# An encoder layer with attention and a Hyena branch on one core: GpSimd's sums ahead of the attention moved to VectorE, and half of the weights' low parts made by an accumulating DMA

## The chip, the cores and the metric

The kernel runs on one core of a Trainium2 chip. The metric is the device time of one execution in microseconds (us), as the median of several runs. A core has TensorE (PE in the profile, with PEld for its weight loads), VectorE (DVE), ScalarE (ACT), GpSimd (POOL) and SyncE (SP). Each engine works through its own list of instructions in order and waits on semaphores for the others. DMAs are issued from the lists of SP, ACT and POOL and run on 16 shared DMA engines.

## The reference, cut to what matters

One layer on x of 512 positions by 1024 features, all in fp32:

```
proj = rmsnorm(x) @ w_in                      # 1024 -> q-latent 768 | kv-latent 256 | rope key 32 | Hyena 1536
q = rmsnorm(c_q) @ w_uq ; k, v = rmsnorm(c_kv) @ w_ukv   # 8 heads, q and k normed, 32 features rotated
y_attn  = softmax(q k^T * s) v
x0, x1, vh = split(dwconv3(u_h))
h_fwd, h_bwd = filters(three sin layers of a small MLP, then filt_w_out)
y_hyena = x0 * (circular convolution of x1*vh with the filters, by FFT)
x = x + concat(rmsnorm(y_attn), rmsnorm(y_hyena)) @ w_out
x = x + (silu(g) * u) @ w_down    with g, u = dwconv3(rmsnorm(x) @ w_up)
x = x + sigmoid(x @ w_ple_gate) * rmsnorm(p @ w_ple)
```

## The kernel before, in words

Features lie on the 128 partitions and the 512 positions along the free dimension. To keep fp32 accuracy, every operand of a large product is split in two: a high part, rounded to the fp32r format that TensorE reads, and a low part, the operand minus that. A product of K tiles is three matmuls for each tile: high by high, high by low and low by high (`prod3`).

**Weights** come as tiles of 128 x 1024 (w_uq: 128 x 768), in the order in which TensorE uses them (`stream`): 21 of w_in, one of w_ukn, six of w_uq, one of w_ukv, eight of w_out, then w_up, w_down, w_ple and w_gate. `wload` (L134) brings one in: SP loads the raw tile `wr` (L136), ScalarE rounds it into `wh` (L139), and the low part `wl` is the difference. The table CUTS gives for each of the first 37 tiles the column up to which VectorE subtracts (L141); GpSimd takes the rest (L143). There are three buffers for `wr` and two each for `wh` and `wl`; when TensorE starts on tile i, tiles up to i+1 have been ordered (L167). So a tile may be prepared once TensorE has left the tile two ahead of it. From w_up on, VectorE makes all of `wl`.

**Stages.** 1. x is loaded, scaled and split, and its sum of squares is gathered in accx and accy (L485 to L491), on GpSimd for even k and on VectorE for odd k. 2. `in_gemm` (L310) runs the 21 tiles of w_in: kv-latent, rope key, then eight Hyena tiles whose short convolution (`conv`, L532) is on ScalarE and VectorE, and whose products x1*vh (`uu`) and their sums (`pq`) are on GpSimd (L625 to L629), four more Hyena tiles, and six of the q-latent, whose squares are summed in accx (L645). 3. Between them run tasks: the filter network (`filter_task`, L394) with three sin layers (L367 on TensorE, L370 to L372 on VectorE, L374 on ScalarE), the sums of the two halves of filt_w_out (L403, GpSimd; the loaded tile takes a `wr` buffer), and the filters (L436); the transforms (`transform_task`, L545): sums at L574 to L577, products with the filters at L586 to L591, sums at L595, L596 and L607. 4. The products with w_ukn and w_uq, the squares of each head (`square`, L650) and the scales (`key_task`, `query_scale`; rows are turned by TensorE at L228), rotations (`rotate`, L353). 5. Attention, eight heads by four blocks of 128 queries, the normalization by GpSimd (L866), with the values, the inverse transform and the first parts of w_out between. 6. w_out, the gated MLP and the last gate.

**What sets the order.** TensorE's order is written out by the program: a clock counts the cost of the matmuls written so far, and a task goes on when its time has come (`advance`, `spawn`). The lists of the other engines are ordered by a list scheduler with priorities, from the program order and its own estimates. The table ENG names the engine for single operations by a key, and `e(key, default)` looks it up.

The functions that the change touches and what calls them, with the line numbers of the profile:

Of the kernel before, what the change touches and what calls it, by code (L numbers as in the profile page):

```python
# [12 lines left out]
F32 = mybir.dt.float32  # L13
# [33 lines left out]
D_FT = 3.5  # L47
CUTS = [0, 0, 1024, 256, 512, 512, 256, 768, 256, 768, 256, 0, 512, 0, 256, 256, 768, 256, 512, 0, 256, 512, 0, 512, 768, 512, 768, 768, 0, 256, 256, 256, 0, 256, 0, 512, 512]
TAIL = 'E0 P E1 R O S0 S1 V0 V1 S2 S3 V2 G0 V3'
ENG = {'pr0': 'G', 'a53': 'V', 'a64': 'V', 'sp3': 'V', 'pr2': 'G', 'sp7': 'G', 'qa2': 'V', 'm5': 'V', 'a51': 'G', 'ah1': 'G', 'hl0': 'V', 'fwo': 'G', 'ah3': 'G', 'qa5': 'V', 'hl2': 'G', 'qa3': 'V', 'm6': 'V', 'm7': 'G', 'm2': 'V', 'qa1': 'V', 'sp5': 'G', 'xt': 'V', 'Uc': 'G', 'sp4': 'G', 'w01': 'V', 'w11': 'V', 'a61': 'G', 'pr3': 'G', 'a67': 'G', 'a63': 'V', 'u4': 'G', 'a65': 'G', 'w10': 'G', 'u3': 'G', 'sp0': 'G', 'eos': 'V', 'vx': 'A', 'vl': 'V', 'vh': 'V', 'va': 'V', 'vf': 'V', 've': 'V', 'vc': 'A', 'sx': 'A', 'sl': 'V', 'sh': 'V', 'sa': 'V', 'sf': 'V', 'se': 'V', 'sc': 'V', 'qa4': 'G', 'sp6': 'V', 'm4': 'V', 'rot2': 'G', 'cv5': 'V', 'm1': 'G', 'a62': 'V', 'rot1': 'G'}  # L50
PRI = {'val': 20, 'kt': 60, 'rms': -120, 'cols': 400, 'H': 0, 'gate': 150, 'uT': -120, 'io': -20, 'sq': 20, 'turn': 0, 'so': -300, 'fold': -120, 't8': 0, 'gsq': -50, 'ie': 400}
QACT = 1
# [34 lines left out]
def tile_encoder_block(  # L87
# [6 lines left out]
    V, S, G, PE, SP = nc.vector, nc.scalar, nc.gpsimd, nc.tensor, nc.sync  # L94

    def e(key, default):
        return {"V": V, "G": G}[ENG.get(key, default)]

# [24 lines left out]
    def f32(ap):  # L123
        return ap.bitcast(F32)
# [9 lines left out]
    def wload(src, n, cut):  # L134
        raw = wpool.tile([P, 1024], F32, tag="wr", name="wr", bufs=3)
        SP.dma_start(raw[:, :n], src)  # L136
        hi = wpool.tile([P, 1024], F32R, tag="wh", name="wh")
        lo = wpool.tile([P, 1024], F32R, tag="wl", name="wl")
        S.activation(hi[:, :n], raw[:, :n], AF.Copy)  # L139
        if cut:  # L140
            V.tensor_tensor(lo[:, :cut], raw[:, :cut], f32(hi[:, :cut]), op=ALU.subtract)  # L141
        if cut < n:
            G.tensor_tensor(lo[:, cut:n], raw[:, cut:n], f32(hi[:, cut:n]), op=ALU.subtract)  # L143
        return hi, lo

    stream = [(w_in[m], 1024, CUTS[m]) for m in range(21)]
    stream += [(w_ukn, 1024, CUTS[21])] + [(w_uq[m], 768, CUTS[22 + n]) for n, m in enumerate(UQ)] + [(w_ukv, 1024, CUTS[28])]
    stream += [(w_out[1, m], 1024, CUTS[29 + m]) for m in range(4)] + [(w_out[0, m], 1024, CUTS[33 + m]) for m in range(4)]
    stream += [(w_up[m], 1024, 1024) for m in range(2 * NFF)]
# [8 lines left out]
    def ahead(i):  # L158
        while len(ready) < min(i, len(stream)):
            with tc.high_priority(offset=WPRI if len(ready) > 3 else 0):  # L160
                ready.append(wload(*stream[len(ready)]))

    def next_w():
        i = taken[0]
        taken[0] += 1
        if i:
            ahead(i + 2)  # L167
        return ready[i]
# [89 lines left out]
    def first_tile():  # L258
        return [
            wpool.tile([P, 1024], dt, tag=g, name=g, bufs=n)  # L260
            for g, dt, n in (("wr", F32, 3), ("wh", F32R, 2), ("wl", F32R, 2))
        ]
# [60 lines left out]
    sel = const.tile([P, 56], F32R, tag="sel", name="sel")  # L323
    selT = const.tile([40, 6, P], F32R, tag="selT", name="selT")

# [68 lines left out]
    def filter_task():  # L394
# [3 lines left out]
        fw_hl = []  # L398
        fwo = wpool.tile([P, 1024], F32, tag="wr", name="wr", bufs=3)
        SP.dma_start(fwo, fw_out)  # L400
# [82 lines left out]
    for k in range(8):  # L483
        sq = (accx, accy)[k] if k < 2 else tmp()
        S.activation(sq, xraw[k], AF.Square)  # L485
        if k >= 2:
            if k % 2 == 0:
                last = G.tensor_tensor(accx, accx, sq, op=ALU.add)
            else:
                V.tensor_tensor(accy, accy, sq, op=ALU.add)  # L490
    V.tensor_tensor(accx, accx, accy, op=ALU.add)  # L491
# [3 lines left out]
    SP.dma_start(ident, c_id)  # L495
    with tc.issue_after(last.ins):
        for i in (0, 1):
            G.dma_start(dft[i], c_dft[i])
        G.dma_start(sel, c_sel)
        G.dma_start(selT, c_selT)  # L500
        for i in (2, 3):
            G.dma_start(dft[i], c_dft[i])
        G.memset(f32(t8), 0.0)
# [146 lines left out]
    def square(src):  # L650
        with pri("sq"):
            sq = single("sq")
            S.activation(sq, src, AF.Square)
            h, l = tmp(F32R), tmp(F32R)
            split(h, l, sq)
        return h, l
# [416 lines left out]
    def embedding():  # L1073
        ptr = wpool.tile([P, 1024], F32, tag="wr", name="wr", bufs=3)
        SP.dma_start(ptr, pT)
# [220 lines left out]
```

## Time and profile before

| | us |
|---|---|
| median of 3 runs (774.09 to 775.78) | 775.2 |
| the profiled execution | 776.35 |
| its span, first to last instruction | 774.6 |
| busy: TensorE matmul / VectorE / ScalarE / GpSimd | 730.1 / 520.8 / 359.8 / 246.2 |
| mean granted TensorE clock | 0.982 |

How to read it. The page gives for each engine its busy time, and for each group of instructions the line, engine, operation, output and inputs by name, their count, summed time and mean; behind the bar stands the engine's idle time just ahead of them and what ended it ("<-ACT wh L139": an instruction of ScalarE at L139 that wrote wh). A timeline row is start, duration, engine, line and operation, with the idle time before it in brackets. A row of the table by stretches has the stretch, its length, and for PE, PEld, DVE, ACT and POOL the busy time and the count, then the granted TensorE clock as a share of full speed, the DMA engines' busy share and GB/s. A matmul row counts from its issue to its modelled end, so successive rows overlap; at full clock one of 128x512 follows the other by 5.44/24 = 0.227 us. Instructions of one shape on VectorE overlap a little too: rows of 0.68 us start 0.60 us apart.

### The profile page before, as it was taken

How to read it: one execution, taken by the hardware profiler on the slowest of the kernel's cores; microseconds unless marked ns; L12 is line 12 of the kernel's file. 1: busy time of each engine (PE TensorE's matmuls, PEld its weight loads, DVE VectorE, ACT ScalarE, POOL GpSimd, SP SyncE). 2: the span in 40 equal slices, each digit the busy share in tenths (PEclk: the TensorE clock that was granted, in tenths of full speed). 3: DMA queues.
4: the chain of work that ended last, by engine and by line, in shares of the span. 5: the costliest groups of instructions: out<-in, count | busy, mean ns of one | idle time of the engine just before them, and what ended most of it. 6: DMA issues, size and time to landing. Idle time of an engine off the chain costs nothing.

```text
span 774.6 us, 8970 instructions
## 1 busy us (share of the span) xinstructions
PE 730.1 (94%) x3254; PEld 585.1 (76%) x3254; DVE 520.8 (67%) x721; ACT 359.8 (46%) x546; POOL 246.2 (32%) x201
## 2 busy tenths in 40 slices
PE   6995999988798989999999999999999999999997
PEld 4773788765567777777888888888888888888886
DVE  6476998899878989786866656566565333233383
ACT  6452443334757978354554443434444122226341
POOL 4335542567355665232232122212222000005000
PEclk9997999989899999999999999999999999999999
DMA  8622332211243310022323232332223323333331
GB/s 278 214 82 82 109 109 82 67 50 41 83 128 103 96 49 28 33 98 89 99 90 109 83 108 86 105 105 86 106 84 103 95 84 107 93 125 102 108 109 55
DMA packets 25502, 74.83 MB, mean 97 GB/s; under 512 B 3401, under 2 KB 3977, under 8 KB 25458
## 3 DMA queue, kind: packets, MB, share of 16 engines
q1 hardware_dynamic: 24418, 71.62, 28.3%
q0 software_dynamic: 784, 2.25, 0.9%
q8 instruction: 25, 0.41, 0.2%
q10 hardware_dynamic: 256, 0.39, 0.2%
q14 instruction: 19, 0.16, 0.1%
HBM read 69.01 MB, written 2.10 MB: 92 GB/s over the span
## 4 chain that ended last, share of the span: by engine, by line
PE 53%; DVE 0%; ACT 0%; DVEq 0%; issue 0%
PE mm L173 36%; PE ax L173 17%; PE ax L217 0%; DVE t L1124 0%; ACT t L1123 0%; DVEq L1291 0%; DVE t L1125 0%
## 5 line engine op out<-in xcount | busy, mean ns | idle before, releaser
L173 PE MATMUL mm<-a,wh 128*128 128x512 f32 (+1 forms) x928 | 290.6, 394 | 8.8 <-ACT wh L270 5.5
L173 PEld LDWEIGHTS mm<-a,wh 128*128 128x128 f32 x928 | 175.0, 191 | 52.6 <-ACT wh L270 5.5
L141 DVE TENSOR_TENSOR wl<-wr,wh 128x1024 fp32r<-128x1024 f32 (+3 forms) x106 | 128.4, 1211 | 115.6 <-ACT wh L139 104.4
L139 ACT ACTIVATE wh<-wr 128x1024 fp32r<-128x1024 f32 (+1 forms) x113 | 116.3, 1029 | 156.2 <-PE mm L173 105.4
L173 PE MATMUL mm<-a,wl 128*128 128x512 f32 (+1 forms) x464 | 181.4, 391 | 1.0 <-DVE wl L141 1.0
L173 PE MATMUL ax<-a,wh 128*128 128x512 f32 x384 | 118.3, 389 | 0.0
L173 PEld LDWEIGHTS mm<-a,wl 128*128 128x128 f32 x464 | 88.5, 191 | 19.6 <-DVE wl L141 1.4
L143 POOL TENSOR_TENSOR wl<-wr,wh 128x768 fp32r<-128x768 f32 (+3 forms) x31 | 58.1, 1875 | 83.5 <-ACT wh L139 79.3
L173 PEld LDWEIGHTS ax<-a,wh 128*128 128x128 f32 x384 | 72.1, 188 | 14.9
L1060 POOL TENSOR_TENSOR f<-f 128x512 f32<-128x512 f32 x22 | 28.7, 1303 | 169.5 <-DVE f L540 149.9
L173 PE MATMUL ax<-a,wl 128*128 128x512 f32 x192 | 74.7, 389 | 0.0
L173 PE MATMUL mm<-g,wh 128*128 128x512 f32 x232 | 73.7, 399 | 0.6 <-ACT t L644 0.6
L173 PE MATMUL mm<-h,wh 128*128 128x512 f32 x192 | 59.0, 389 | 0.0
L173 PEld LDWEIGHTS mm<-g,wh 128*128 128x128 f32 x232 | 44.1, 192 | 12.7 <-issue 1.9
L173 PE MATMUL mm<-g,wl 128*128 128x512 f32 x116 | 46.1, 397 | 1.5 <-DVE wl L141 1.5
L1091 POOL TENSOR_TENSOR acc<-acc,t 128x512 f32<-128x512 f32 x7 | 10.0, 1436 | 102.9 <-ACT t L1090 102.4
L173 PEld LDWEIGHTS ax<-a,wl 128*128 128x128 f32 x192 | 36.0, 188 | 7.6
L173 PEld LDWEIGHTS mm<-h,wh 128*128 128x128 f32 x192 | 36.0, 188 | 7.5
L1056 DVE TENSOR_TENSOR f<-mm,R 128x512 f32<-128x512 f32 x22 | 15.2, 691 | 33.9 <-PE mm L173 33.9
L173 PE MATMUL mm<-h,wl 128*128 128x512 f32 x96 | 37.3, 389 | 0.0
L533 ACT ACTIVATE f<-f,par 128x512 f32<-128x512 f32 x44 | 35.5, 808 | 0.7 <-DVE f L1056 0.7
L540 DVE SCALAR_TENSOR_TENSOR f<-f,par 128x511 f32<-128x511 f32 x44 | 33.8, 771 | 1.4
(311 smaller groups left out, 1068.7 us busy)
## 6 DMA issues: line engine op xcount, KB each, us to landing
wr<-in_w_up_dram SPq DMA_DIRECT2D x44, 512.0 KB, 3.5
wr<-in_w_in_dram SPq DMA_DIRECT2D x19, 512.0 KB, 3.2
wr<-in_w_down_dram SPq DMA_DIRECT2D x16, 512.0 KB, 3.5
x<-in_xT_dram SPq DMA_DIRECT2D x16, 256.0 KB, 3.3
wr<-in_w_out_dram SPq DMA_DIRECT2D x8, 512.0 KB, 3.7
wr<-in_w_gate_dram SPq DMA_DIRECT2D x8, 512.0 KB, 3.5
wr<-in_w_down_dram SPq DMA_DIRECT2D x8, 384.0 KB, 3.0
wr<-in_w_uq_dram SPq DMA_DIRECT2D x6, 384.0 KB, 3.0
```

Of the source, the lines that this page charges most:

```text
L139: S.activation(hi[:, :n], raw[:, :n], AF.Copy)
L141: V.tensor_tensor(lo[:, :cut], raw[:, :cut], f32(hi[:, :cut]), op=ALU.subtract)
L143: G.tensor_tensor(lo[:, cut:n], raw[:, cut:n], f32(hi[:, cut:n]), op=ALU.subtract)
L173: last = PE.matmul(out, l, r, start=start and i == 0, stop=stop and i == n - 1)
L533: S.activation(c, z, AF.Identity, scale=pcol(w, 3 * m + 1), bias=pcol(b, m))
L540: V.scalar_tensor_tensor(c[:, 0 : T - 1], z[:, 1:T], pcol(w, 3 * m + 2), c[:, 0 : T - 1], op0=ALU.mult, op1=ALU.add)
L1056: V.tensor_tensor(z, ps_up.pop(m), R2, op=ALU.mult)
L1060: G.tensor_tensor(cc[1], cc[0], cc[1], op=ALU.mult)
L1091: G.tensor_tensor(acc7, acc7, sq, op=ALU.add)
```

## The change

It does four things, all ahead of or around the attention.

1. `e()` gives GpSimd only to the keys of the set ATT (pr, a, ah, hl, xt), which are used in and behind the attention. All other keyed operations now run on VectorE: the products `uu` and `pq`, the sums of filt_w_out, the rotations, the sums and products of the transforms, the sum of squares of the q-latent. Of the sums of squares of x GpSimd keeps one (k = 6), behind which its loads of the transform matrices still stand.
2. A low part is made in two ways: VectorE subtracts the first columns (all 1024 for the first five tiles, then 512, or 384 of w_uq's 768), and for the rest ScalarE writes the negated rounded part into `wl` and GpSimd issues a DMA that adds the weights from HBM onto it. CUTS is gone.
3. `wr` has two buffers in place of three, `wh` and `wl` three in place of two, and tiles up to i+2 are ordered when TensorE starts on tile i.
4. The squares in `square` are written to accy, in place of a tile of their own, and selT lies in another pool, which makes room.

```diff
-CUTS = [0, 0, 1024, 256, 512, 512, 256, 768, 256, 768, 256, 0, 512, 0, 256, 256, 768, 256, 512, 0, 256, 512, 0, 512, 768, 512, 768, 768, 0, 256, 256, 256, 0, 256, 0, 512, 512]
+ATT = {'pr', 'a', 'ah', 'hl', 'xt'}
...
     def e(key, default):
-        return {"V": V, "G": G}[ENG.get(key, default)]
+        if key.rstrip("0123456789") in ATT:
+            return {"V": V, "G": G}[ENG.get(key, default)]
+        return V
...
     def wload(src, n, cut):
-        raw = wpool.tile([P, 1024], F32, tag="wr", name="wr", bufs=3)
+        raw = wpool.tile([P, 1024], F32, tag="wr", name="wr", bufs=2)
         SP.dma_start(raw[:, :n], src)
-        hi = wpool.tile([P, 1024], F32R, tag="wh", name="wh")
-        lo = wpool.tile([P, 1024], F32R, tag="wl", name="wl")
+        hi = wpool.tile([P, 1024], F32R, tag="wh", name="wh", bufs=3)
+        lo = wpool.tile([P, 1024], F32R, tag="wl", name="wl", bufs=3)
         S.activation(hi[:, :n], raw[:, :n], AF.Copy)
-        if cut:
-            V.tensor_tensor(lo[:, :cut], raw[:, :cut], f32(hi[:, :cut]), op=ALU.subtract)
+        V.tensor_tensor(lo[:, :cut], raw[:, :cut], f32(hi[:, :cut]), op=ALU.subtract)
         if cut < n:
-            G.tensor_tensor(lo[:, cut:n], raw[:, cut:n], f32(hi[:, cut:n]), op=ALU.subtract)
+            S.activation(lo[:, cut:n], raw[:, cut:n], AF.Copy, scale=-1.0)
+            G.dma_start(lo[:, cut:n], src[:, cut:n], accum_op=ALU.add)
         return hi, lo
...
-    stream = [(w_in[m], 1024, CUTS[m]) for m in range(21)]
+    stream = [(w_in[m], 1024, 1024 if m < 5 else 512) for m in range(21)]
+    stream += [(w_ukn, 1024, 512)] + [(w_uq[m], 768, 384) for m in UQ] + [(w_ukv, 1024, 512)]
+    stream += [(w_out[g, m], 1024, 512) for g in (1, 0) for m in range(4)]
...
         if i:
-            ahead(i + 2)
+            ahead(i + 3)
...
         if k >= 2:
-            if k % 2 == 0:
-                last = G.tensor_tensor(accx, accx, sq, op=ALU.add)
-            else:
-                V.tensor_tensor(accy, accy, sq, op=ALU.add)
+            acc = (accx, accy)[k % 2]
+            last = (G if k == 6 else V).tensor_tensor(acc, acc, sq, op=ALU.add)
+            if k == 6:
+                gate_consts = last
...
     def square(src):
         with pri("sq"):
-            sq = single("sq")
-            S.activation(sq, src, AF.Square)
+            S.activation(accy, src, AF.Square)
             h, l = tmp(F32R), tmp(F32R)
-            split(h, l, sq)
+            split(h, l, accy)
```

The changed kernel's lines stand three further on (two from L649 on). TensorE's list is the same in both.

First place: ScalarE's list at the second and third sin layer. Before (t read at L128 is a sum of filt_w_out, x written at L374 a sin layer's result):

```order
L131 ACTIVATE ckh_172<-x,par 128x512
L139 ACTIVATE wh<-wr 128x1024
L128 ACTIVATE g<-t 128x512
L374 ACT_TABLE_LOAD
L374 ACTIVATE x<-t 128x512
L128 ACTIVATE g<-t 128x512
L533 ACTIVATE t<-t,par 128x512 x2
```

And now:

```order
L145 ACTIVATE wl<-wr 128x512
L536 ACTIVATE t<-t,par 128x512
L377 ACT_TABLE_LOAD
L377 ACTIVATE x<-t 128x512
L142 ACTIVATE wh<-wr 128x1024
L131 ACTIVATE g<-t 128x512
L145 ACTIVATE wl<-wr 128x512
L536 ACTIVATE t<-t,par 128x512
```

The second sin layer's result stood behind the rounding of a sum of filt_w_out, and now stands ahead of it; the negated low parts (L145) are new in the list.

Second place: VectorE's list from the end of the second sin layer (L372, now L375) to the start of the third (L370, now L373). Before:

```order
L372 SCALAR_TENSOR_TENSOR t<-t 128x512
L618 TENSOR_TENSOR t<-mm,R_189 128x512
L129 TENSOR_TENSOR g<-t,g 128x512
L618 TENSOR_TENSOR t<-mm,R_189 128x512
L129 TENSOR_TENSOR g<-t,g 128x512
L534 SCALAR_TENSOR_TENSOR t<-t,par 128x511 x2
L540 SCALAR_TENSOR_TENSOR t<-t,par 128x511
L141 TENSOR_TENSOR wl<-wr,wh 128x768
L540 SCALAR_TENSOR_TENSOR t<-t,par 128x511
L370 TENSOR_SCALAR t<-ax,par,turns 128x512
```

And now the first rows of that stretch:

```order
L375 SCALAR_TENSOR_TENSOR t<-t 128x512
L628 TENSOR_TENSOR uu_178<-t 128x256
L629 TENSOR_TENSOR uu_178<-t 128x128
L630 TENSOR_TENSOR uu_178<-t 128x128
L406 TENSOR_TENSOR t<-wr 128x512
L631 TENSOR_TENSOR pq_164<-uu_178 128x128
L632 TENSOR_TENSOR pq_164<-uu_178 128x128
L406 TENSOR_TENSOR t<-wr 128x512
L621 TENSOR_TENSOR t<-mm,R_189 128x512
L215 SCALAR_TENSOR_TENSOR t<-t 128x512
L143 TENSOR_TENSOR wl<-wr,wh 128x512
L132 TENSOR_TENSOR g<-t,g 128x512
```

GpSimd's products uu and pq and the two sums of filt_w_out (L406) have come in, and a weight's low part (L143) stands behind them, whose raw tile takes the buffer that filt_w_out leaves.

More of the change, by code (lines that the diff above doesn't have):

```diff
@@ L134, in wload @@
     def wload(src, n, cut):
-        raw = wpool.tile([P, 1024], F32, tag="wr", name="wr", bufs=3)
+        raw = wpool.tile([P, 1024], F32, tag="wr", name="wr", bufs=2)
         SP.dma_start(raw[:, :n], src)
-        hi = wpool.tile([P, 1024], F32R, tag="wh", name="wh")
-        lo = wpool.tile([P, 1024], F32R, tag="wl", name="wl")
+        hi = wpool.tile([P, 1024], F32R, tag="wh", name="wh", bufs=3)
+        lo = wpool.tile([P, 1024], F32R, tag="wl", name="wl", bufs=3)
         S.activation(hi[:, :n], raw[:, :n], AF.Copy)
-        if cut:
-            V.tensor_tensor(lo[:, :cut], raw[:, :cut], f32(hi[:, :cut]), op=ALU.subtract)
+        V.tensor_tensor(lo[:, :cut], raw[:, :cut], f32(hi[:, :cut]), op=ALU.subtract)
         if cut < n:
-            G.tensor_tensor(lo[:, cut:n], raw[:, cut:n], f32(hi[:, cut:n]), op=ALU.subtract)
+            S.activation(lo[:, cut:n], raw[:, cut:n], AF.Copy, scale=-1.0)
+            G.dma_start(lo[:, cut:n], src[:, cut:n], accum_op=ALU.add)
         return hi, lo
-    stream = [(w_in[m], 1024, CUTS[m]) for m in range(21)]
-    stream += [(w_ukn, 1024, CUTS[21])] + [(w_uq[m], 768, CUTS[22 + n]) for n, m in enumerate(UQ)] + [(w_ukv, 1024, CUTS[28])]
-    stream += [(w_out[1, m], 1024, CUTS[29 + m]) for m in range(4)] + [(w_out[0, m], 1024, CUTS[33 + m]) for m in range(4)]
+    stream = [(w_in[m], 1024, 1024 if m < 5 else 512) for m in range(21)]
+    stream += [(w_ukn, 1024, 512)] + [(w_uq[m], 768, 384) for m in UQ] + [(w_ukv, 1024, 512)]
+    stream += [(w_out[g, m], 1024, 512) for g in (1, 0) for m in range(4)]
     stream += [(w_up[m], 1024, 1024) for m in range(2 * NFF)]
@@ L260, in first_tile @@
             wpool.tile([P, 1024], dt, tag=g, name=g, bufs=n)
-            for g, dt, n in (("wr", F32, 3), ("wh", F32R, 2), ("wl", F32R, 2))
+            for g, dt, n in (("wr", F32, 2), ("wh", F32R, 3), ("wl", F32R, 3))
         ]
@@ L323, in tile_encoder_block @@
     sel = const.tile([P, 56], F32R, tag="sel", name="sel")
-    selT = const.tile([40, 6, P], F32R, tag="selT", name="selT")
+    selT = single("selT", (40, 6, P), F32R)
     tasks, clock, serial = [], [0.0], itertools.count()
@@ L398, in filter_task @@
         fw_hl = []
-        fwo = wpool.tile([P, 1024], F32, tag="wr", name="wr", bufs=3)
+        fwo = wpool.tile([P, 1024], F32, tag="wr", name="wr", bufs=2)
         SP.dma_start(fwo, fw_out)
@@ L495, in tile_encoder_block @@
     SP.dma_start(ident, c_id)
-    with tc.issue_after(last.ins):
+    with tc.issue_after(gate_consts.ins):
         for i in (0, 1):
@@ L1073, in embedding @@
     def embedding():
-        ptr = wpool.tile([P, 1024], F32, tag="wr", name="wr", bufs=3)
+        ptr = wpool.tile([P, 1024], F32, tag="wr", name="wr", bufs=2)
         SP.dma_start(ptr, pT)
```

## The prediction

> **What bounds the kernel now.** I read the page, then the busy times by stretches, the waits of TensorE (PE), and the timelines about them. The table by stretches, and a tile's matmuls from the chain that ended last:
>
> ```profile
> 0.00:245.00 245.00, 215.73 (x872) 161.41 (x872) 195.87 (x270) 120.67 (x194) 118.93 (x96) 0.94 0.32 107
> 358.50:774.60 416.10, 410.85 (x1830) 340.30 (x1830) 223.15 (x259) 160.83 (x205) 67.40 (x51) 1.00 0.30 97
> ```
> ```profile
> 371.08 5.44 PE ax L173 x24
> ```
>
> From 358.5 on PE is busy 410.85 of 416.1 us at full clock, and the change alters there only the buffers: nothing to gain. Ahead of the attention (about 0 to 245) PE idles 245.0 - 215.7 = 29.3 us and its clock is 0.94, while VectorE (DVE) works 195.9 us. The waits of PE in that stretch:
>
> ```profile
> PE ax L367 <- ACT x L374: 8.1, 1, 8.1
> PE mm L173 <- DVE wl L141: 5.6, 4, 3.2
> PE mm L173 <- ACT wh L270: 5.5, 1, 5.5
> PE ax L228 <- ACT t L664: 5.0, 2, 4.3
> PE ax L173 <- DVE g L411: 1.4, 1, 1.4
> PE mm L173 <- ACT t L644: 0.6, 1, 0.6
> ```
>
> The 5.5 is the start and stays. Three long ones are each followed by a slow clock:
>
> ```profile
> 67.60:74.50 6.90, 6.87 (x14) 4.30 (x15) 4.05 (x6) 2.97 (x4) 1.20 (x1) 0.50 0.16 61
> 171.00:177.00 6.00, 6.00 (x15) 4.75 (x16) 6.00 (x6) 2.97 (x5) 4.82 (x3) 0.51 0.21 66
> 201.10:207.90 6.80, 6.80 (x17) 4.16 (x18) 6.20 (x16) 5.41 (x12) 0.00 (x0) 0.52 0.22 77
> ```
>
> At half clock, half of each is lost: 3.4, 3.0 and 3.3 us. So 21 us of waits and 10 of clock can be won ahead of the attention, no more.
>
> **Why DVE is late.** One and the same product, first beside a busy GpSimd (POOL), then beside an idle one (timeline of DVE):
>
> ```profile
> 171.40 0.68 DVE L587 TENSOR_TENSOR t<-g,x 128x512 f32<-128x512 f32 x1
> 172.00 0.68 DVE L590 TENSOR_TENSOR g<-g,x 128x512 f32<-128x512 f32 x1
> 172.60 1.76 DVE L588 TENSOR_TENSOR g<-g,x 128x512 f32<-128x512 f32 x1
> ...
> 182.09 0.68 DVE L588 TENSOR_TENSOR g<-g,x 128x512 f32<-128x512 f32 x1
> ```
>
> POOL worked on accx from 172.18 and on a low part from 173.78:
>
> ```profile
> 172.18 1.63 POOL L645 TENSOR_TENSOR accx<-accx,t 128x512 f32<-128x512 f32 x1 [2.52 <-ACT t L644]
> 173.78 2.26 POOL L143 TENSOR_TENSOR wl<-wr,wh 128x768 fp32r<-128x768 f32 x1
> ```
>
> **Part 1, the sums to DVE.** They are 52 of POOL's instructions, of which these are the largest group and that of the products uu:
>
> ```profile
> L607 POOL TENSOR_TENSOR t<-g 128x512 f32<-128x512 f32 x5 | 8.6, 1749 | 2.5 <-DVE a L129 2.4
> L625 POOL TENSOR_TENSOR uu<-t 128x256 f32<-128x256 f32 x4 | 4.7, 1176 | 12.2 <-DVE t L540 12.2
> ```
>
> By the diff 32 are of 512 columns, 4 of 256, 16 of 128. Successive DVE rows of 512 start 0.60 us apart (171.40, 172.00, 172.60); halves and quarters in proportion, with some overhead, 0.35 and 0.20: 32 x 0.60 + 4 x 0.35 + 16 x 0.20 = 24 us. DVE's columns of low parts grow by 3,328 up to w_ukv (14,592 against 11,264 in CUTS), at 1.2 us per 1,024 (next row) 4 us: 28 us in all. Against it stands the stretching. Taking each of DVE's 270 rows at the duration that its shape has beside an idle POOL (0.68, 0.74 with a scalar, 1.23 for 1,024 columns), I get 162 of 210 us summed: 48 us go. So DVE's work falls by some 20 us although it takes POOL's.
>
> ```profile
> 21.23 1.23 DVE L141 TENSOR_TENSOR wl<-wr,wh 128x1024 fp32r<-128x1024 f32 x1 [0.35 <-ACT wh L139]
> ```
>
> **The filter network** is the first place. Timeline of ACT, PE and DVE:
>
> ```profile
> 65.01 0.63 ACT L128 ACTIVATE g<-t 128x512 fp32r<-128x512 f32 x1 [7.83 <-POOL t L403]
> 65.66 1.28 ACT L374 ACT_TABLE_LOAD   x1
> 66.95 0.63 ACT L374 ACTIVATE x<-t 128x512 f32<-128x512 f32 x1
> ```
> ```profile
> 67.63 2.07 PE L367 MATMUL ax<-x 64*128 64x512 f32 x2 [8.08 <-ACT x L374]
> ...
> 84.49 1.65 PE L173 MATMUL ax<-g 128*128 128x512 f32 x6 [1.40 <-DVE g L411]
> ```
> ```profile
> 51.59 1.07 DVE L212 SCALAR_TENSOR_TENSOR t<-t 128x512 f32<-128x512 f32 x1
> ...
> 58.03 0.81 DVE L370 TENSOR_SCALAR t<-ax,par,turns 128x512 f32<-128x512 f32 x1
> ```
>
> Now the sin stands ahead of the rounding that waited for POOL. And of the nine rows between 51.59 and 58.03 only a low part still stands ahead of the layer's first row, so that it begins near 53.5, a little over the 51.59, and its three rows, with two of conv between, end at 57. The result is there at 58, ahead of PE (67.63 - 8.08 = 59.5): the 8.1 us go. But next is late what hung on it. From there DVE has 35 rows (the eight among them) to the third layer's last one (L411): uu, pq, L403, conv, two low parts, at 0.2 to 0.75 us each 19 us. Twice it waits: 3 us for a raw tile, which can only be loaded (3.2 us) when L403 has left its buffer, and 1 us for ACT. L411 ends at 57 + 19 + 4 = 80, where PE, no longer held, arrives at about 72. A wait of 8 us takes the place of that of 8, one place on; the first filter product starts at 80 in place of 84.5, and half clock follows it to about 87, in place of 67.6 to 74.5, and costs 3.4 again, now behind 80. Gain: 4.5 - 3.4 = **1.1 us** (-3 to 8: the 35 rows may go faster, or wait more).
>
> **Part 2, low parts.** VectorE's half is ready earlier, and three buffers leave two tiles (10.9 us) in place of one. The waits at low parts and the two about them:
>
> ```profile
> 148.38 0.50 PE L173 MATMUL mm<-a,wl 128*128 128x512 f32 x1 [0.95 <-DVE wl L141]
> 170.87 0.80 PE L173 MATMUL mm<-ckh,wl 128*128 128x512 f32 x1 [3.15 <-DVE wl L141]
> 179.62 0.73 PE L173 MATMUL mm<-g,wh 128*128 128x512 f32 x2 [0.65 <-ACT t L644]
> 185.23 0.50 PE L173 MATMUL mm<-g,wl 128*128 128x512 f32 x1 [0.62 <-DVE wl L141]
> 192.99 0.49 PE L173 MATMUL mm<-g,wl 128*128 128x512 f32 x1 [0.85 <-DVE wl L141]
> ```
>
> ```profile
> 72.17 1.06 ACT L139 ACTIVATE wh<-wr 128x1024 fp32r<-128x1024 f32 x1 [2.66 <-PE mm L173]
> ```
>
> They go: 0.95 + (3.15 + 3.0 of clock) + 0.65 + 0.62 + 0.85 = **9.2 us** (5 to 9.5). The second half's chain, from PE's leaving a buffer: ACT's rounding 1.06, its negation 0.63 (as L128's copy above), then the DMA, of which no row exists. The nearest rows are POOL's plain loads of 512 KB, and SP's of a weight tile:
>
> ```profile
> DMA to landing us min/median/max: 4.7/6.3/7.7
> ```
> ```profile
> wr<-in_w_in_dram SPq DMA_DIRECT2D x19, 512.0 KB, 3.2
> ```
>
> An accumulating one of 256 KB reads its target too: 3.2 to 7.7 us, I take 5, nearest to the median with half the bytes. PE needs that half 2 x 5.44 + 2.72 = 13.6 us after it left the buffer, and 1.7 + 5 + some 3 of queueing is 9.7: hidden, also at 7.7. POOL's list waits on ACT at each such DMA; behind it stands nothing but the next. One was issued in 0.55 us while DVE worked:
>
> ```profile
> 18.83 0.55 POOL L499 DMA_DIRECT2D sel<-in_c_sel_dram  x1
> ```
> ```profile
> 18.74 0.74 DVE L132 SCALAR_TENSOR_TENSOR a<-x,gm,a 128x512 fp32r<-128x512 f32 x1
> ```
>
> [...]
>
> ACT's 25 negations (0.6 us, 15 in all) lie in its idle time (120.7 busy of 245), but one stands ahead of L202 and delays R1: **-0.6 us**.
>
> **The scales.** The wait of 4.3, and w_ukn's last matmul:
>
> ```profile
> 178.58 0.40 PE L173 MATMUL mm<-ckh,wl 128*128 128x512 f32 x1
> ...
> 201.09 0.59 PE L228 MATMUL ax<-ident,t 8*128 8x8 f32 x4 [4.30 <-ACT t L664]
> ```
>
> ACT's L664 stands behind the splits of eight sums (L607), five of them POOL's at 1.7 us. Now DVE makes all. After PE's start on w_ukn it is about 4 us to the split of the first square, then 29 rows of 0.6 us, 17.4, and 1.2 for ACT: 22.6. PE comes by after 5.4 for w_ukn and 196.8 - 178.8 = 18.0 less 2.4 of waits that go, 21.0. Some 1.6 to 3 remain; I take 2.5. That is under 3.15, the shortest wait above that cost the clock, and over 1.4, which did not; I take the clock as kept: 1.8 + 3.3 = **5.1 us** (0 to 7.6). The other wait at L228 goes, 5.0 - 4.3 = **0.7**.
>
> **Attention and rest.** DVE's low parts there grow by 2,048 columns (2.4 us), ACT's by eight negations; POOL's low parts, which stretched others, go. I take 0 (-2 to 4). At the start two sums of 0.68 move to DVE, which waits for ACT there: 0 (-0.7 to 0).
>
> **The sum**: 1.1 + 9.2 - 0.6 + 5.1 + 0.7 = 15.5 us. The profiled execution took 776.35 (span 774.6 and 1.75 around it), 1.15 above the median 775.2: 760.8 by its own, 759.7 by the median. I say **760**.
>
> **Rivals.** (a) All these waits go: 21 + 10, less R1's 0.6: 775.2 - 30 = 745. For: DVE is 20 us lighter. Against: the count of rows to L411. (b) Only the low parts help; new waits of over 3.15 us at L411 and at the scales keep their clocks: 1.1 + 9.2 - 0.6 - 3 of further waits = 7 us, 768. For: one list in order on DVE, now with POOL's rows. (c) Slower: the accumulating DMA lands late. A buffer's cycle is 1.7 + L + 2.7 us (1.06 + 0.63; half a tile's matmuls, 2.72), three buffers share it, so the period is (4.4 + L)/3, over 5.44 from L = 11.9 us on. At 15 it is 6.5, 1.0 more for each of 24 tiles: 25 - 16 = 9 us slower, 784; even at L = 13.9. Against: the rows of 3.2 to 7.7. (d) DVE becomes the bound, the stretching having another cause: +28 us in a stretch where it works 195.9 of 245; beyond what idle time takes up, some 20 us, 795. [...]
> (e) The change does nothing: DVE's gain is used up in its list, 775.
>
> **How the numbers follow.** Chances: forecast 0.50, (a) 0.12, (b) 0.20, (c) 0.07, (d) 0.04, (e) 0.07. 760 with its own terms' spread reaches 752 to 766; (b) adds to 770, and half of (a) down to 749: with 772 above, this range leaves out (c), (d), (e) and some of (a), about 2 in 10. A difference of 0.2% (1.5 us) is about what a measurement of this kernel can tell. Faster: the forecast, (a) and (b), 0.82 with a little of (e), 0.84; same 0.05; slower 0.11.
>
> **What would show it.** Right: DVE's rows of 512 columns at 0.68 throughout to the attention, no wait at L367 (now L370), one of 5 to 10 us at the first filter product (L414) with half clock behind it, none at low parts, under 3 us at L231. Wrong: PE waiting for a DMA of wl, each tile's start more than 5.44 us behind the last; stretched DVE rows beside DMAs; a filter wait of over 12 us or none.

## The result, and the profile after

The changed kernel took 757.43 us (median of 4 runs, 756.98 to 758.01), the kernel before 775.49 beside it: the ratio is 0.9772, 95% interval 0.9759 to 0.9785, 18.1 us less. The forecast was 760, with a range of 749 to 772. The sum held; two of its terms did not. The profiled execution has a span of 755.3 us, 19.3 less than the one before.

Where TensorE gained them, by the start of the same matmul in both traces (its order is the same in every kernel of this study, so that any two traces can be compared row by row):

| matmul on TensorE | before | after | ahead by |
|---|---|---|---|
| sums for R1 (L217, now L220) | 40.77 | 40.11 | 0.7 |
| first filter product | 84.49 | 73.68 | 10.8 |
| first of the transforms (g, dft) | 103.2 | 93.9 | 9.3 |
| last of them | 151.9 | 141.3 | 10.6 |
| R1's transposes (ident, R) | 196.4 | 177.1 | 19.3 |
| the query's scale (L228, now L231) | 201.1 | 182.1 | 19.0 |
| last of (a, dft) | 232.7 | 214.1 | 18.6 |
| last of (ks, qs) | 305.6 | 288.1 | 17.5 |
| end of the span | 774.6 | 755.3 | 19.3 |

TensorE's longest waits now, with total, times and longest:

```profile
PE mm L176 <- ACT wh L273: 5.6, 1, 5.6
PE ax L231 <- ACT t L666: 5.3, 2, 4.6
PE ax L176 <- DVE ptl L132: 3.3, 2, 2.9
PE ax L176 <- DVE g L414: 2.6, 1, 2.6
```

Ahead of the attention the wait of 8.1 at the second sin layer and all those at low parts are gone. One of 2.6 us has come at the filter product, where the forecast had one, of 8. The wait at the scales stayed. The rows of both, and the clock behind them:

```profile
73.68 2.90 PE L176 MATMUL ax<-g 128*128 128x512 f32 x6 [2.61 <-DVE g L414]
182.06 0.59 PE L231 MATMUL ax<-ident,t 8*128 8x8 f32 x4 [4.60 <-ACT t L666]
```
```profile
73.60:76.00 2.40, 2.32 (x6) 1.87 (x7) 2.22 (x4) 0.81 (x1) 0.00 (x0) 0.50 0.47 179
182.00:186.00 4.00, 3.94 (x10) 1.92 (x11) 3.22 (x9) 2.71 (x8) 0.00 (x0) 0.50 0.37 131
```

VectorE's work up to the same matmul (the last of (a, dft)), in the trace before and then in the one after. The columns are busy time and count of PE, weight loads, DVE, ACT, POOL, then clock, DMA share and GB/s:

```profile
0.00:232.70 232.70, 203.96 (x814) 151.94 (x815) 185.26 (x241) 111.66 (x171) 113.63 (x90) 0.94 0.33 110
```
```profile
0.00:214.10 214.10, 196.94 (x813) 148.36 (x814) 171.38 (x296) 124.61 (x197) 28.28 (x40) 0.97 0.58 150
```

VectorE has 55 rows more and works 13.9 us less.

### The profile page after: what moved, and what is told of

It reads as the page before. It is cut to its first block, busy times and chain, and to the rows that moved or that the text cites. A ratio compares the mean times of both kernels' runs of the same rounds, so it can differ in the third digit from the quotient of the medians.

```text
span 755.3 us, 9041 instructions
## 1 busy us (share of the span) xinstructions
PE 723.2 (96%) x3254; PEld 581.8 (77%) x3254; DVE 503.5 (67%) x780; ACT 375.4 (50%) x578; POOL 151.7 (20%) x150
## 4 chain that ended last, share of the span: by engine, by line
PE 54%; DVE 0%; ACT 0%; DVEq 0%; issue 0%
PE mm L176 37%; PE ax L176 17%; PE ax L220 0%; DVE t L1126 0%; ACT t L1125 0%; DVE t L1127 0%; DVEq L1293 0%
## 5 line engine op out<-in xcount | busy, mean ns | idle before, releaser
L176 PE MATMUL mm<-a,wh 128*128 128x512 f32 (+1 forms) x928 | 288.1, 391 | 7.6 <-ACT wh L273 5.6
L143 DVE TENSOR_TENSOR wl<-wr,wh 128x1024 fp32r<-128x1024 f32 (+3 forms) x113 | 124.3, 1101 | 115.2 <-ACT wh L142 113.3
L176 PE MATMUL mm<-a,wl 128*128 128x512 f32 (+1 forms) x464 | 179.6, 387 | 0.0
L1061 ACT ACTIVATE f<-f 128x512 f32<-128x512 f32 x22 | 13.9, 631 | 44.5 <-DVE f L543 44.5
L146 POOL DMA_DIRECT2D wl<-in_w_in_dram x16 | 13.9, 868 | 106.2 <-DVE wl L143 46.0
L543 DVE SCALAR_TENSOR_TENSOR f<-f,par 128x511 f32<-128x511 f32 x44 | 33.9, 771 | 1.4
```

Of the source, the lines that this page charges most:

```text
L146: G.dma_start(lo[:, cut:n], src[:, cut:n], accum_op=ALU.add)
L176: last = PE.matmul(out, l, r, start=start and i == 0, stop=stop and i == n - 1)
L543: V.scalar_tensor_tensor(c[:, 0 : T - 1], z[:, 1:T], pcol(w, 3 * m + 2), c[:, 0 : T - 1], op0=ALU.mult, op1=ALU.add)
L1061: S.activation(cc[0], cc[0], AF.Silu)
```

## The experiments

Twelve kernels were run, each beside the kernel before on the same chip. Ratios are to that kernel, with a 95% interval.

### Each part alone

The sums alone (from the kernel before):

```
+        if key.rstrip("0123456789") not in ATT:
+            return V
         return {"V": V, "G": G}[ENG.get(key, default)]
...
+            last = (G if k == 6 else V).tensor_tensor(acc, acc, sq, op=ALU.add)
```

> The kernel before with part 1 alone: GpSimd's 52 sums ahead of the attention go to VectorE, the weights' low parts and the buffers stay as they were. Theory (GpSimd's arithmetic stretches VectorE's rows, and both parts are needed to end that): GpSimd's low parts still stretch some 40% of VectorE's rows, which now are more; the wait at the second sin layer (8.1 us) goes since nothing waits for GpSimd there, the low parts' waits stay or grow; 766 us (762 to 772). Rival (the low parts and the buffers gave all of it, the sums are only more work for VectorE): no gain, 775 to 780 us.

The low parts and buffers alone (from the changed kernel):

```
-        if key.rstrip("0123456789") in ATT:
-            return {"V": V, "G": G}[ENG.get(key, default)]
-        return V
+        return {"V": V, "G": G}[ENG.get(key, default)]
...
-            last = (G if k == 6 else V).tensor_tensor(acc, acc, sq, op=ALU.add)
+            last = (G if k % 2 == 0 else V).tensor_tensor(acc, acc, sq, op=ALU.add)
```

> The changed kernel with the 52 sums back on GpSimd: accumulating DMA, three pairs of buffers, VectorE's half of each low part stay. Theory: the waits at low parts and the clock behind them go (9.2 us), the filter's wait of some 8 us at the second sin layer and the scales' of 4 stay, since GpSimd's sums are as slow as they were: 766 us (763 to 769). Rival (the low parts and the buffers gave all of it): 757 to 759 us.

Measured: the sums alone 763.0 us, ratio 0.9853 (0.9837 to 0.9870); the low parts alone 766.7, ratio 0.9904 (0.9889 to 0.9919). The rival fails in both: each part is worth something, 12 and 8 us, and together 18. The sums are worth more than I expected: the waits at low parts, which were to stay or grow, fell from 5.6 us to 2.3. The low parts alone came out at the expected time, but not by the expected account: the wait at the second sin layer, which was to stay at 8.1 us, is 0.77 there, since GpSimd, rid of low parts, starts on the sums of filt_w_out at 56.17 and not at 63.72. The filter product and the query's scale, for the sums alone and then for the low parts alone:

```profile
75.00 2.93 PE L176 MATMUL ax<-g 128*128 128x512 f32 x6 [4.82 <-DVE g L414]
187.14 0.59 PE L231 MATMUL ax<-ident,t 8*128 8x8 f32 x4 [4.07 <-ACT t L667]
```
```profile
76.02 1.66 PE L174 MATMUL ax<-g 128*128 128x512 f32 x6 [1.85 <-DVE g L412]
190.22 0.41 PE L229 MATMUL ax<-ident,t 8*128 8x8 f32 x4 [3.83 <-ACT t L664]
```

At the filter product (84.49 before, 73.68 after) either part alone brings 8.5 to 9.5 of the 10.8 us: what one does there the other need not do again. The second half tells them apart: at the scales the sums are 14.0 us ahead and the low parts 10.9, and both together 19.0.

### Is it GpSimd's work that holds up VectorE?

In the changed kernel GpSimd adds up pieces of the rounded weights for nobody:

```
-            G.dma_start(lo[:, cut:n], src[:, cut:n], accum_op=ALU.add)
+            G.dma_start(lo[:, cut:n], src[:, cut:n], accum_op=ALU.add); [G.tensor_tensor(idle, f32(hi[:, c : c + 256]), f32(hi[:, c : c + 256]), op=ALU.add) for c in range(0, 1024 if len(ready) < 22 else 0, 256)]
```

> The changed kernel, and GpSimd adds four quarters of each rounded weight tile to itself, into a tile that nobody reads, for 17 weight tiles: 66 instructions of 256 columns, some 45 us of GpSimd ahead of 160 us. Nobody waits for their result; the orders of the other engines are the same. Theory (a busy GpSimd stretches VectorE): GpSimd's extra work is 45 of the 74 us that the change took away, so of the 48 us of stretching some 29 come back, rows of 512 columns take 1.2 to 1.8 us beside it, and some 6 of the 18 us of gain are lost or more: 763 to 768 us. Rival (what counted was that engines waited for GpSimd's results): 757 to 759 us.

Measured: 778.0 us, ratio 1.0038 (1.0027 to 1.0050). The whole gain is lost, and 3 us beyond, more than I had expected, though nobody reads those sums. VectorE's rows, and GpSimd's beside them:

```profile
68.56 1.55 DVE L543 SCALAR_TENSOR_TENSOR t<-t,par 128x511 f32<-128x511 f32 x1
...
75.00 1.49 DVE L374 TENSOR_SCALAR t<-t 128x512 f32<-128x512 f32 x1
```
```profile
62.21 5.89 POOL L146 TENSOR_TENSOR idle<-wh 128x256 f32<-128x256 f32 x4 [2.91 <-ACT wh L142]
...
75.30 1.66 POOL L146 TENSOR_TENSOR idle<-wh 128x256 f32<-128x256 f32 x2
```

The same two rows take 0.74 and 0.41 us in the changed kernel. Two groups of VectorE's up to 245 us (count, busy time, mean ns; idle time before them), the second with a matmul's output as one of its inputs:

```profile
L543 DVE SCALAR_TENSOR_TENSOR t<-t,par 128x511 f32<-128x511 f32 x8 | 8.4, 1050 | 0.1
L621 DVE TENSOR_TENSOR t<-mm,R 128x512 f32<-128x512 f32 x12 | 8.2, 682 | 3.5 <-PE mm L176 3.5
```

L621 keeps its 682 ns, as in the trace of the change. TensorE's wait at the filter product becomes 9.1 us, much what the forecast had. One wait for the sums themselves there is, since they read `wh` and so hold its buffer:

```profile
94.90 1.06 ACT L142 ACTIVATE wh<-wr 128x1024 fp32r<-128x1024 f32 x1 [3.75 <-POOL idle L146]
```

Half of the loss, 10.1 us, lies ahead of it: the filter product starts at 83.75, against 73.68. GpSimd's DMAs stood behind those sums too. So a second run keeps GpSimd as busy with instructions that read nothing:

```
-            G.dma_start(lo[:, cut:n], src[:, cut:n], accum_op=ALU.add)
+            d = G.dma_start(lo[:, cut:n], src[:, cut:n], accum_op=ALU.add)
+            with tc.issue_after(d.ins): [G.memset(idle, 1.0) for _ in range(10 if len(ready) < 22 else 0)]
```

> The changed kernel, and behind each accumulating DMA of 17 weight tiles GpSimd fills a tile that nobody reads, ten times 256 columns (170 instructions, some 50 us by 0.57 us for the 512 columns of the fill at 19.55 us of the changed kernel): GpSimd is as busy as in the run with added sums, its DMAs stand behind as much, but it reads nothing. The orders of the other engines are the same. Theory (it is GpSimd's reading of two tiles that VectorE's rows wait beside): VectorE's rows stay at 0.68 us, 757 to 760 us. Second (any work of GpSimd stretches VectorE): 768 to 778 us, with rows of over 1 us. Third (the run with added sums was slow because its DMAs were issued late behind them): 768 to 778 us, with rows of 0.68 us.

Measured: 757.75 us, ratio 0.9775 (0.9751 to 0.9800), the time of the changed kernel. GpSimd's fills, and VectorE's rows beside them (in this kernel lines from there on count one higher, so that L544 is L543 above and L375 is L374):

```profile
59.50 3.97 POOL L147 MEMSET idle<- 128x256 f32 x10
63.73 0.86 POOL L146 DMA_DIRECT2D wl<-in_w_in_dram  x1 [0.27 <-DVE t L544]
64.28 4.32 POOL L147 MEMSET idle<- 128x256 f32 x10
```
```profile
62.85 0.74 DVE L544 SCALAR_TENSOR_TENSOR t<-t,par 128x511 f32<-128x511 f32 x1
...
66.42 0.44 DVE L375 TENSOR_SCALAR t<-t 128x512 f32<-128x512 f32 x1
```

Up to 245 us GpSimd is busy 98.6 us here and 93.8 in the run with sums. Neither its being busy nor its DMAs' place behind other work costs anything (757.75 us against 757.43); what is left is what the sums do and the fills do not: they add tiles, read from SBUF, beside VectorE's rows.

The size fits. For each of VectorE's rows, take what it lasts beyond the median of its operation and shape beside an idle GpSimd (rows that read a matmul's output apart, and from 0.06 us on), and add this up to the last of (a, dft). That gives 43.1 us in the kernel before, 19.8 with the sums alone moved, 29.0 with the low parts alone, 2.2 in the changed kernel and with the fills, and 19.5 with the idle sums, which cost 20.6 us of time. Of these 19.5, 10.0 lie ahead of the filter product.

Not every row was held up beside the sums. L543, with two tiles as inputs, took 1050 ns on the mean, against 744 in the changed kernel and beside the fills. L374, with one tile, took 1.49 us at 75.00, and 0.44 beside the fills. L621, with a tile and a matmul's output, kept its 682 ns. VectorE's rows from 63.52 to 66.60 kept 0.67 us too, beside the four sums that took 5.89 us, where two took 1.66 at 75.30. What decides which side is held up, no run shows. Beside rows of L374 (L375 in this kernel) two fills were held up. Behind the first of each ten a fill takes 0.31 us, other than the two that start while such a row runs:

```profile
53.78 0.42 DVE L375 TENSOR_SCALAR t<-t 128x512 f32<-128x512 f32 x1
```
```profile
53.94 0.50 POOL L147 MEMSET idle<- 128x256 f32 x1
...
54.50 0.31 POOL L147 MEMSET idle<- 128x256 f32 x1
...
66.45 0.66 POOL L147 MEMSET idle<- 128x256 f32 x1
```

Both start behind the row (53.78 and 66.42) and end 0.25 us after it. A fill that was just ending when the row at 53.78 started cost the row nothing: it took 0.42 us, as in the changed kernel.

### Buffers, and the low parts without the DMA

The kernel before with the buffers alone:

```
-        raw = wpool.tile([P, 1024], F32, tag="wr", name="wr", bufs=3)
+        raw = wpool.tile([P, 1024], F32, tag="wr", name="wr", bufs=2)
...
+        lo = wpool.tile([P, 1024], F32R, tag="wl", name="wl", bufs=3)
...
-            ahead(i + 2)
+            ahead(i + 3)
```

> The kernel before with the buffers alone: three pairs of rounded and low parts, two raw tiles, the weights taken one tile further ahead; GpSimd's sums and low parts as before. Theory (what the low parts gained came from GpSimd's arithmetic going, not from the buffers): the waits at low parts go (0.95 to 3.15 us, 5.6 in all, and 3 us of clock) but those at the filter (8.1) and the scales stay: 768 to 772 us. Rival (the buffers make no difference while GpSimd is slow): 775 us. Third (the buffers gave all that the low parts gave, 8.4 us): 766.7 us.

Measured: ratio 1.0044 (1.0028 to 1.0060), 3.4 us slower. Buffers are no part of the gain by themselves (part 4 of the change, which makes room for them, is in this kernel too); none of the three expectations had it slower. Where the 3.4 us went is not shown.

VectorE makes every low part whole:

```
-        V.tensor_tensor(lo[:, :cut], raw[:, :cut], f32(hi[:, :cut]), op=ALU.subtract)
-        if cut < n:
-            S.activation(lo[:, cut:n], raw[:, cut:n], AF.Copy, scale=-1.0)
-            G.dma_start(lo[:, cut:n], src[:, cut:n], accum_op=ALU.add)
+        V.tensor_tensor(lo[:, :n], raw[:, :n], f32(hi[:, :n]), op=ALU.subtract)
```

> The changed kernel without the accumulating DMA and the negations: VectorE makes each low part whole, 32 x 0.6 us more, 15 us of it ahead of the attention. Theory (VectorE's list decides where TensorE waits): four of these stand ahead of the filter product and four ahead of the scales, 2.4 us each, and the wait at each grows by that, with more half clock; 762 us (759 to 766). Rival (the DMA's share is what hides least, or VectorE has room): 755 to 758 us.

Measured: 768.3 us, ratio 0.9925 (0.9905 to 0.9946), 11 us slower than with the DMA. That the DMA earns its place was expected; the place was not. There is no wait at the filter product, but one a little later, and the query's scale is 3.6 us behind the changed kernel:

```profile
102.20 0.66 PE L550 MATMUL ax<-ident,uu 128*128 128x128 f32 x4 [3.88 <-DVE t L436]
...
185.62 0.59 PE L228 MATMUL ax<-ident,t 8*128 8x8 f32 x4 [4.87 <-ACT t L663]
```

The other 7 us are lost behind that, in and after the attention, where TensorE waits for splits of activations (L134 and L135, 3.5 and 3.2 us) and its clock is 0.96 from 217.5 to 294.1 (in the changed kernel 1.00 over the same matmuls).

### Where the late sums belong

The sums of the transform and the squares of the queries stay on GpSimd, those ahead of them go to VectorE:

```
-ATT = {'pr', 'a', 'ah', 'hl', 'xt'}
+ATT = {'pr', 'a', 'ah', 'hl', 'xt', 'Uc', 'Us', 'm', 'sp', 'qa'}
```

> The changed kernel, in which the sums behind 135 us (of the transform, its eight sums and the squares of the queries, 25 or so of 512 columns) stay on GpSimd as before, and those ahead of it (filter, products uu and pq, rotations, first squares) are on VectorE. Theory: up to the end of the filter's transforms it runs as the changed kernel (10.6 us gained by 141 us); behind that the stretching comes back, the gain of the next stage (8.4 us) falls to 1 to 3: 763 us (761 to 766). Rival (the late sums are better off on GpSimd, since VectorE's list decides the scales' wait): 752 to 757 us.

Measured: 765.8 us, ratio 0.9884 (0.9865 to 0.9903). As expected, it keeps step with the changed kernel to the last transform (141.2 against 141.3) and then falls back by 6.6 us up to the query's scale. The stretching is back there: summed as above, 14.3 us between these two matmuls, where the changed kernel has none. TensorE's waits:

```profile
165.54 0.73 PE L176 MATMUL mm<-g,wh 128*128 128x512 f32 x2 [2.29 <-ACT t L647]
180.28 0.59 PE L176 MATMUL ax<-t,sel 128*8 128x512 f32 x1 [2.40 <-DVE t L132]
188.67 0.41 PE L231 MATMUL ax<-ident,t 8*128 8x8 f32 x4 [2.95 <-ACT t L666]
```

### Less for VectorE, more for the DMA

```
-    stream = [(w_in[m], 1024, 1024 if m < 5 else 512) for m in range(21)]
+    stream = [(w_in[m], 1024, 1024 if m < 5 else 256) for m in range(21)]
...
```

> The changed kernel with three quarters of each low part (512 of 768 columns for w_uq) by negation and accumulating DMA up to w_ukv, and a quarter by VectorE, which has 7 us less to do ahead of the attention; ScalarE has 7 us more. Theory (VectorE's list decides, and the accumulating DMA is hidden by far): the filter product's low half comes 1 to 1.5 us earlier, the scales' row 1 us earlier, no wait for a low part: 754 us (751 to 756). Rival (the DMA of 384 KB lands late, or ScalarE's negations hold up its list): 757 to 765 us, with waits for wl.

Measured: 767.1 us, ratio 0.9900 (0.9874 to 0.9926): the theory fails, and so does the rival's reason. TensorE waits for no low part, though the DMA of 384 KB lands after 6.6 us in place of 5.4. What is late is another transfer. SyncE's list (L139 is a weight tile's load, L432 one of the decay table), then VectorE's wait from 60 to 125 us and TensorE's for that row:

```profile
86.38 14.77 SPq L139 DMA_DIRECT2D wr<-in_w_in_dram  x3
101.20 0.91 SPq L432 DMA_DIRECT2D t<-in_c_dec_dram  x2
```
```profile
DVE t L439 <- DMA t<-in_c_dec_dram: 4.5, 3, 2.0
...
PE ax L553 <- DVE t L439: 5.3, 2, 3.2
```

Moved low parts changed the order of the loads: the decay table now stands behind three weight tiles, whose loads wait for buffers, and VectorE stands still for it, and TensorE behind that. These 5.3 us, and 6.8 us at half clock behind them (from 108.23), are the largest share of the 10 that are lost; at the query's scale it is 7.9 behind (189.96).

### What holds the scales

TensorE waited 4.6 us for ScalarE's copy L666. That copy's input, L673, was done at about 173.3; the copy ran at 181.44. Two reorderings, both from the changed kernel. The query's copy ahead of some splits:

```
-            split(h, l, t)
+            late.append((h, l, t)) if n >= 3 else split(h, l, t)
...
-        q, r1 = rows(ps), col("r1")
+        q, r1 = rows(ps), col("r1"); [split(*late.pop(0)) for _ in range(len(late))]
```

> The changed kernel; ScalarE's copy of the query's sums (L666) now stands behind four of the eight splits of the transform's sums, not behind all eight (the last five splits are written out behind that copy). TensorE's order is the same. Theory (TensorE's wait of 4.6 us at L231 is ScalarE's and VectorE's list, which holds a copy whose input was there by 173): the copy runs some four pairs of 1.2 us earlier, the wait falls to under 1 us and the half clock behind it (182 to 190 us, 3.7 us lost) goes: 750 us (748 to 753). Rival (behind that wait TensorE waits for the next row of the same lists, the key's scales): 755 to 758 us.

Measured: 758.0 us, ratio 0.9785 (0.9768 to 0.9801): no gain, as the rival had it. The wait went from the query's copy, and the same wait came at the keys':

```profile
175.60 0.57 ACT L666 ACTIVATE t<-ax 8x512 f32<-8x512 f32 x1
...
184.64 0.57 ACT L666 ACTIVATE t<-ax 8x512 f32<-8x512 f32 x1
```
```profile
176.57 1.02 PE L689 MATMUL ax<-qr,ones 32*8 32x512 f32 x2
...
185.26 0.47 PE L231 MATMUL ax<-ident,t 8*128 8x8 f32 x4 [4.71 <-ACT t L666]
```

The keys' copy has its input at 177.6 and runs 7 us later, behind rows of ScalarE's list that wait for VectorE. So both go ahead:

```
-        k = rows(ssk)
+        k = rows(ssk); [split(*late.pop(0)) for _ in range(len(late))]
...
+        with tc.high_priority(offset=5000): S.activation(r, ps[0:8, :], AF.Copy)
```

> The changed kernel; the last five splits of the transform's sums are now written out behind ScalarE's second copy of a scale row (L666, for the keys), and both copies have a higher priority. TensorE's order is the same. In the run before with the query's copy ahead, that wait went and one of 4.7 us came at the keys' copy, whose input was there at 177.6 and which ran at 184.6. Theory (ScalarE's order of its list holds up copies that could run, not the amount of work): the keys' copy runs some 4 us earlier, the wait there falls to 1 or 2 us and the clock behind it is kept: 753 us (750 to 755). Rival (VectorE's list is the bound there, TensorE waits at the next row): 757 us, with a wait of 4 us somewhere behind 176.

Measured: 752.64 us, ratio 0.9713 (0.9696 to 0.9729): the theory holds, and this is faster than both kernels (its interval lies clear below that of the change). The query's scale starts at 178.11, 4.0 us ahead of the changed kernel. The wait that is left, at the keys':

```profile
184.16 0.41 PE L231 MATMUL ax<-ident,t 8*128 8x8 f32 x4 [1.74 <-ACT t L666]
```

### The filter's place in VectorE's list

The third sin layer's low half ahead of two rows, alone and with the first of the scales' reorderings:

```
-        S.activation(hs, h, AF.Copy)
-        V.tensor_tensor(hs[64:128, :], h[64:128, :], f32(hs[64:128, :]), op=ALU.subtract)
+        with tc.high_priority(offset=600): S.activation(hs, h, AF.Copy)
+        with tc.high_priority(offset=600): V.tensor_tensor(hs[64:128, :], h[64:128, :], f32(hs[64:128, :]), op=ALU.subtract)
```

> The changed kernel with the third sin layer's low half (L414) ahead of two other rows of VectorE (L135), 1.4 us earlier. Theory: the wait of 2.6 us at the first filter product falls to 1.2, which is under every wait behind which the clock fell, so that the half clock behind it (1.4 us lost) goes too: 754.6 us (753 to 756.5). Rival (what TensorE gains there it waits for at the next rows of VectorE's list): 757 us.

> The two reorderings together (the filter's low half and the query's sums). Theory: the gains add, 757.4 - 7.4 - 2.8 = 747 us (745 to 751). Rival (VectorE's list of 200 us in 245 is the bound, and each gain is waited for at the next place): 753 to 757 us.

Measured: 760.9 us, ratio 0.9817 (0.9803 to 0.9832), and 760.5, ratio 0.9810 (0.9796 to 0.9825): both slower than the change, by some 3 us, which no theory and no rival had. The wait at the filter product fell to 1.22 and 1.21, as meant, and the first transform came 1.75 us earlier than in the changed kernel with the filter's reordering alone (92.16 against 93.91). But the scheduler moved other rows of VectorE and ScalarE too, and three new waits came at the products' transposes, 2.8 to 2.9 us in all, with half clock behind them; at the last transform the two kernels are 2.9 and 3.4 us behind. With both reorderings the keys' copy is waited for as well (4.35 us). From the kernel with the filter's alone:

```profile
73.41 1.66 PE L176 MATMUL ax<-g 128*128 128x512 f32 x6 [1.22 <-DVE g L414]
101.99 0.66 PE L553 MATMUL ax<-ident,uu 128*128 128x128 f32 x4 [1.53 <-DVE x L393]
```

## Why the prediction was right, and where it was not

**What bounds it, and the stretching: right.** The forecast's root was that VectorE's rows of 0.68 us take up to 1.76 because GpSimd works beside them, so that VectorE gets lighter by taking GpSimd's work. The runs with idle sums and with fills show it for sums (L543 at 1050 ns on the mean beside them), and not for fills (744). The size was too large: 13.9 us less work, where the forecast had 20. The mis-sized term is "162 of 210 us summed: 48 us go". With the median of every shape beside an idle GpSimd the 270 rows sum to 167, so that 44 go, and 28 off that leaves 16. Some 2 us of stretching stay, half of them in a row of 1.73 us at 15.01, beside the one sum of squares that GpSimd keeps.

**The filter: 1.1 us forecast, 8.6 gained** (9.3 less the 0.7 at R1). The wait moved from the second sin layer to the first filter product, as forecast; its size failed. The failing step is VectorE's waits there: "Twice it waits: 3 us for a raw tile", and 1 us for ACT. The count of its rows held: they are 35 and took 18.2 us, where the forecast had 19. They also started 1.6 us earlier, at 55.4 and not at 57, since the layer's first row (L373) began at 52.4 and not "near 53.5". The last row of the second sin layer, the second sum of filt_w_out and the filter's low half on VectorE, and the stretch ahead of it (columns as above):

```profile
54.77 0.68 DVE L375 SCALAR_TENSOR_TENSOR t<-t 128x512 f32<-128x512 f32 x1
...
57.32 0.68 DVE L406 TENSOR_TENSOR t<-wr 128x512 f32<-128x512 f32 x1
...
72.85 0.69 DVE L414 TENSOR_TENSOR g<-x,g 64x512 fp32r<-64x512 f32 x1
```
```profile
60.00:73.60 13.60, 11.07 (x48) 8.81 (x48) 13.55 (x26) 6.95 (x10) 1.73 (x2) 1.00 0.76 199
```

VectorE is busy 13.55 of 13.60 us: the two waits did not come. L406 left the raw tile at 58.0, ScalarE rounded the next one at 61.76, and VectorE reached its low part at 63.52, in the order of its list, without standing still. So L414 ends at 73.5 and not at 80, and TensorE, which came by at 71.07 (72 forecast), waited 2.6 us and not 8. The half clock behind it, 3.4 us in the forecast, lasted to 76.92 and cost 1.6.

**The low parts: 9.2 forecast, 10.0 gained** (19.3 less 9.3 in the table above). All four waits at low parts went, with the half clock behind one of them, and that for L644 (0.65) shrank to 0.27. The accumulating DMA, costed at 5 us with bounds of 3.2 and 7.7 and a limit of 11.9, has these rows (GpSimd's issue; queue, size and time to landing):

```profile
L146 POOL DMA_DIRECT2D wl<-in_w_in_dram x16 | 13.9, 868 | 106.2 <-DVE wl L143 46.0
```
```profile
wl<-in_w_in_dram POOLq DMA_DIRECT2D x16, 256.0 KB, 5.4
```

TensorE never waits for it: rival (c) is out by far. Beside VectorE's rows, without a gap between (58.53 to 59.81 for the one at 58.81), the issue takes 0.86 us, where the plain load at 18.83 took 0.55. It came 0.3 us behind the tile's negation (median of 32, 0.8 at most); the 3 us of queueing in the forecast were an estimate that no row shows.

**The scales: 5.1 forecast, 0.7 lost.** The failing step is "after PE's start on w_ukn it is about 4 us to the split of the first square". TensorE began w_ukn at some 156.5; that split ends at 163.6 (L132 at 162.92), 7 us later. ScalarE had the square at 159.0 but rounded it only at 162.17 (L131), behind a row of its list (L647) that waited 2.1 us for VectorE. Then the list ran as forecast, and ScalarE's copy came 25.5 us after that start, not 22.6, where TensorE came by at 21.0, as forecast. So the wait was 4.6 us and not 2.5, and the clock, which the forecast took as kept, fell to half until 189.6. The run with both copies ahead shows that most of it was no matter of work: the copy stood in line without need. I had seen that it "stands behind the splits of eight sums" and priced the line, without asking whether it had to stand there. The second wait at L228 (0.7) stayed at 0.68, as well.

**Start, R1 and the rest: -0.6 forecast, 1.4 gained.** At R1's sums TensorE waits 1.50 us, where it waited 0.55, so that the 0.6 did come; but 1.6 were won at the start. The two waits of 0.8 there shrank to 0.26 and 0.37, new ones of 0.20 to 0.48 took most of that back, and a stretch at half clock that the prediction had not counted, worth 1.7 us, went. In the trace before and then in the one after:

```profile
13.04:16.45 3.41, 3.36 (x7) 2.19 (x8) 3.41 (x5) 3.41 (x7) 1.60 (x2) 0.50 0.87 278
```
```profile
13.00:16.50 3.50, 3.50 (x17) 2.85 (x16) 3.50 (x6) 2.87 (x6) 1.69 (x2) 1.00 1.02 307
```

Behind the scales 1.1 us were lost up to the last (ks, qs) and 1.8 won after it, where a wait of 0.69 us at 313.08 in the trace before went and one of 1.26 at 358.55 shrank to 0.17.

So 0.7 + 8.6 + 10.0 - 0.7 - 1.1 + 1.8 = 19.3 of span, against 15.5. Two terms, wrong by 7.5 and 6.5 us, nearly cancelled: the sum was right with some luck. Of the rivals, (d) and (e) fell with the sign, and (c) with the DMA's rows. Of (b) one half came true, the scales keeping their wait and its clock, and of (a) the other, the filter's gain.

## What to carry to other kernels

- Before pricing a wait behind a list, ask when the late row's input was there: a copy that is ready 7 us before it runs costs a reordering, not less work.
- GpSimd's sums of tiles in SBUF were paid twice here, once on GpSimd and once by VectorE's rows beside them: 68 sums that nobody reads cost 20.6 us. Fills of the same busy time, with the accumulating DMAs among them, cost nothing (757.75).
- In kernels with lists in fixed order, one edit moves rows far from it: an edit that gives VectorE less to do (more by DMA) was 10 us slower, since a table's load fell behind other loads.

## What the hardware showed that I had not expected

I took a wait of under 3.15 us as safe for TensorE's clock. It is not, and a longer one may be. Behind the 2.61 us at the filter product the clock was 0.50 in the changed kernel. At the same place, the run with the query's copy ahead (a wait of 2.62) and the run with more by DMA (3.52), each from the end of its wait:

```profile
73.80:76.00 2.20, 2.12 (x9) 1.80 (x10) 2.09 (x4) 0.82 (x1) 0.00 (x0) 1.00 0.57 220
```
```profile
75.70:78.00 2.30, 2.24 (x10) 1.85 (x11) 2.27 (x5) 0.15 (x1) 0.00 (x0) 1.00 0.48 184
```

Both kept 1.00; and behind the 1.74 us of the fastest kernel it was 0.50 from 184.45 to 187.86. Length alone does not decide.

The traces show what does. In each, that of the buffers alone aside, the stretches at half clock start whole multiples of 3.413 us apart; in the trace before, those from 13.04, 64.25, 170.06 and 200.78 are 15, 31 and 9 times that apart. Each lasts one, two or three times 3.413 us (those four 3.41, 10.24, 6.83 and 6.83), unless the kernel ends first. So in these traces the clock changed at the edges of windows of 3.413 us, whose place against the start of the kernel differs from trace to trace, and what counted was how much idle time fell into one window:

- In the changed kernel the window from 70.10 to 73.51 holds 2.44 us of the wait at the filter product, and half clock starts at 73.51.
- In the run with the query's copy ahead a window ends at 72.82, in the middle of that wait. 1.56 us of idle time fall into one window and 1.05 into the next, and the clock stays. With more by DMA they are 1.86 and 1.66.
- The 1.74 us of the fastest kernel lie in one window, the one that ends at 184.45.

Take all windows at full clock from 10 us on, in every trace but that of the buffers alone, with the idle time between TensorE's rows, whose ends are modelled. All 33 with 1.9 us of idle time or more were followed by half clock, 5 of the 17 between 1.55 and 1.9, and none with less. A wait of 2.6 us cost 1.6 us of clock (2.61, in the changed kernel) or nothing (2.62, with the query's copy ahead), by where the window's edge fell, which was luck here.
